# Products, additions and low parts of a hybrid attention and S5 layer given from VectorE to GpSimd, two squares to ScalarE, and a new order list

## The chip, the cores and the metric

The kernel runs on one core of a Trainium2 chip. A core has five engines, each with its own instruction stream, worked through strictly in order: TensorE (PE in the profile; its weight loads are PEld), VectorE (DVE), ScalarE (ACT), GpSimd (POOL) and SyncE (SP), which here does nothing but start transfers. [...] The metric is the device time of one execution in microseconds (us), median of several runs.

## The reference

One decoder layer over a sequence of 1024 tokens with a model width of 1024, all in 32-bit floats.

```python
mod = silu(c) @ w_ada + b_ada                      # shift, scale, gate
h = rms_norm(x, norm_g) * (1 + scale) + shift
proj = h @ w_in     # q | k, v of three branches | z_a | branch gates | u | z_s
q = rms_norm(q, q_norm_g)
kc = rms_norm(compress(k...)); vc = compress(v...)  # gelu(blocks @ w1) @ w2
# three branches per head: compressed keys, selected blocks, window of 512
attn = g0 * softmax(q kc) vc + g1 * softmax(rope(q) ks) vs + g2 * softmax(rope(q) kw) vw
attn = attn * silu(z_a)
y = gelu(s5_mixer(u, ...))                          # complex diagonal recurrence
ssm = y * sigmoid(y @ glu_w + glu_b) * silu(z_s)
out = x + gate * (concat([attn, ssm]) @ w_out)
```

There are 8 heads of 64 in two key groups. With 16 blocks of 64 tokens and 16 of them chosen, every block is chosen, so the selected branch is plain causal attention.

## The kernel before

The tokens are cut into 8 tiles of 128. The work is a set of jobs (several hundred calls of a few dozen functions), and every job records its instructions per engine instead of issuing them. All of them leave through one helper, `issue` (L371), so every row of the profile shows L372; a row is told by its tile, not by its line. Which instruction comes next is fixed by hand: the string `ORD` (L27) lists job, engine letter and count (`hc37:v` is the next VectorE instruction of head 7 of token tile 3; `p a v g s` are TensorE, ScalarE, VectorE, GpSimd, SyncE), and the loop at L1942 issues them in that order. The list thus sets the order on each engine's own stream and of the transfers that an engine starts. The table `FLG` gives some jobs' instructions to one engine or another, and the strings of `SLOTS` say which buffer of a kind each tile takes, in order of use.

The stages, as they lie in time:

- **Start, 0 to 40 us.** Tiles 0 to 3 of x (`x_72` in the order, jobs `xl_0`) and 4 to 7 (`x_73`, jobs `xl_1`) are loaded by SP. Their squares (`x_squares`, L541) are summed, on VectorE or ScalarE as `FLG` says; `x_rstd` (L549) makes the factor of 4 tiles, `x_scale` (L555) multiplies the rows, and TensorE transposes them (`ptr<-ident,x`). Beside this, `mod_chunk` (L533) multiplies a row block of `w_ada`, 128x1024 (`wada<-wada,sc`, jobs `ma`, `mb`), with silu(c) and sums it on VectorE: 16 such products make shift and scale, after which `h_chunk` (L593) makes h in a high and a low part (`hhi`, `hlo`). The weights of w_in are split in the same way (`wh` high part on ScalarE, `wl` low part). `kvaw`, `kva` are weights and matmuls of the keys and values (`wsp`, `ptp`), `cU` and `u..m` those of the S5 input (`wr`, `wh`, `wl`, `pu`).
- **40 to 400 us.** Projections, compressed keys and values (`hid`, `pcp`), the tables and the scan of S5 (`s5p`, `mats`, `scan`), the projection of q with its norm and its rotation: `rope` (L721) makes two products of a half tile with cos and with sin (`ropeb<-qnl,rq`, 128x512) on VectorE and their difference and sum on GpSimd (`qr<-ropeb`).
- **Attention, from about 280 us on.** The tiles go in the order 0, 1, 2, 3, 7, 6, 5, 4 (`OA`, `OB`; 4 is the last). For a head `head_a` (L1511) has scores on TensorE (`S`), the maximum on VectorE (`st<-S`), the exponential on ScalarE with its sum (`pp<-S,st`). Per two heads, `head_s` (L1566) takes the reciprocal of the sums and multiplies by the branch gates (`st<-st,gcol`, 128x4), both on VectorE. `head_b` (L1573) writes the high part of the scaled weights (`hl<-pp,st`, ScalarE), `head_c` (L1584) the low part (`hl<-pp,st,hl`, VectorE), and SP then starts the transposing transfer (`PT<-hl`). `unit_b` (L1609) multiplies with the values (`po<-V,PT`). `cmp_attn` (L1462) is the compressed branch (`Sc`, `hlc`, partly on GpSimd). `attn_trans` (L1647) makes the low part of the gated attention on GpSimd (`oh<-za,oh`).
- **The S5 gate, some 400 to 450 us.** `glu` (L1333) has 8 pieces: a matmul, a tanh, a load of z_s, one VectorE product and a last one that writes with a strided view (`ps<-tg,zz`, 128x512), on VectorE too. `levels` (L1388) then scales `ps` and `attn_out` may follow.
- **Output.** `out_half` (L1668), 16 times: load of half a tile of x (`xo<-in_x`, 128x512), `po` times gate on VectorE (`o<-po,macc,gate`), addition of x (`o<-o,xo`), store by SP. `FLG` puts 14 of the 16 additions on VectorE and two (`ao21`, `ao40`) on GpSimd. `last_halves` (L1705) does it for the last tile, 4, at the very end.

## Time and profile before

| | before |
|---|---|
| median of 3 runs | 634.07 us (631.87, 634.07, 638.18) |
| profiled execution | 633.32 us |
| its span (first to last instruction) | 631.5 us, mean granted clock 0.988 |
| PE busy | 582.0 us, 92% |
| DVE busy | 519.2 us, 82% |
| ACT busy | 397.2 us, 63% |
| POOL busy | 121.1 us, 19% |

Rows give starts and lengths in us from the start of the span. In a view of waits a row names the waiting engine and its output tile, then the engine and tile that released it, then us in total, times and longest. In a group of instructions the last columns are busy us in total, mean ns of one, and the idle time of the engine just ahead of them with what ended most of it. "SPq" and "POOLq" are the streams that start transfers.

### The profile page before, as it was taken

What the parts mean: (1) busy time and instruction counts of PE and PEld (TensorE: products, weight loads), DVE (VectorE), ACT (ScalarE), POOL (GpSimd) and SP (SyncE); (2) the same over time, 40 slices, a digit from 0 to 9 for tenths busy, and PEclk for the clock granted to TensorE, in tenths of its full rate; (3) what the DMA queues carried; (4) which work ended last, traced back from release to release, by engine and by line L of the source; (5) the groups of instructions that cost most, each with busy time, mean ns of one, the idle gap of its engine ahead of it and who ended that gap; (6) DMA issues with size and microseconds to landing.
All of it is one profiled execution on the core that took longest, in us unless ns stands there. A gap on an engine that the chain in (4) does not pass through costs nothing.

```text
span 631.5 us, 12501 instructions
## 1 busy us (share of the span) xinstructions
PE 582.0 (92%) x4615; PEld 427.1 (68%) x4615; DVE 519.2 (82%) x1050; ACT 397.2 (63%) x776; POOL 121.1 (19%) x158
## 2 busy tenths in 40 slices
PE   2599999999999999999999999976999998999893
PEld 0378887788889877888887766545456666556561
DVE  5899896979945686987978899979888989887863
ACT  3586533457443235545989998769857777876750
POOL 0114143121392000333121002001111102010200
PEclk9999999999999999999999999998799999999998
DMA  8999223344566525354656799999999999999996
GB/s 316 385 354 256 49 74 114 91 150 115 154 156 218 161 46 138 114 147 166 175 138 153 165 201 214 214 234 281 241 191 210 256 202 220 188 208 206 219 194 213
DMA packets 211695, 118.85 MB, mean 188 GB/s; under 512 B 159601, under 2 KB 189041, under 8 KB 211634
## 3 DMA queue, kind: packets, MB, share of 16 engines
q1 hardware_dynamic: 208706, 113.05, 73.9%
q0 software_dynamic: 2928, 5.00, 3.6%
q8 instruction: 36, 0.59, 0.4%
q14 instruction: 25, 0.20, 0.1%
HBM read 57.05 MB, written 17.56 MB: 118 GB/s over the span
## 4 chain that ended last, share of the span: by engine, by line
PE 67%; DMA 13%; DVE 11%; ACT 3%; issue 3%; SPq 2%; POOL 0%; POOLq 0%; ACTq 0%; DVEq 0%
PE pcp L372 21%; PE ptp L372 13%; PE po L372 12%; DMA PT<-hl 6%; PE S L372 6%; DVE st L372 2%; PE py L372 2%; PE ph L372 2%; DVE hl L372 2%; SPq L372 2%; PE pk L372 2%; PE pu L372 1%; ACT hl L372 1%; PE pc L372 1%; PE pg L372 1%
## 5 line engine op out<-in xcount | busy, mean ns | idle before, releaser
L372 DVE SCALAR_TENSOR_TENSOR hl<-pp,st,hl 128x640 f16<-128x640 f32 (+7 forms) x128 | 95.3, 765 | 17.4 <-ACT hl L372 16.3
L372 ACT ACTIVATE hl<-pp,st 128x640 f16<-128x640 f32 (+7 forms) x128 | 89.8, 731 | 25.5 <-DMA PT<-hl 11.4
L372 ACT ACTIVATE pp<-S,st 128x640 f32<-128x640 f32 (+7 forms) x128 | 88.7, 697 | 25.2 <-DVE st L372 15.3
L372 PE MATMUL po<-wo,oh 128*128 128x512 f16 x384 | 91.4, 379 | 4.1 <-DVE o L372 2.3
L372 DVE TENSOR_REDUCE st<-S 128x1 f32<-128x640 f32 (+7 forms) x96 | 84.1, 883 | 5.5 <-PE S L372 4.8
L372 PE MATMUL pcp<-hhi,wh 128*128 128x512 f32 x208 | 85.5, 411 | 0.0
L372 PE MATMUL ptp<-wsp,hhi 128*128 128x512 f32 x256 | 83.3, 407 | 0.0
L372 PE MATMUL pcp<-hlo,wh 128*128 128x512 f32 x208 | 82.0, 394 | 0.0
L372 PE MATMUL pcp<-hhi,wl 128*128 128x512 f32 x208 | 81.9, 394 | 0.0
L372 PE MATMUL S<-kT,qg 128*128 128x512 f16 (+3 forms) x384 | 74.6, 319 | 2.1 <-ACT pp L372 2.1
L372 PEld LDWEIGHTS <-PT 128*128 128x128 f16 x1584 | 60.4, 99 | 19.0 <-DMA PT<-hl 8.0
L372 PE MATMUL po<-V,PT 128*128 128x64 f16 x1584 | 66.6, 194 | 6.3 <-DMA PT<-hl 6.3
L372 PEld LDWEIGHTS <-oh 128*128 128x128 f16 x384 | 34.7, 98 | 38.9 <-issue 4.0
L372 PEld LDWEIGHTS ptp<-wsp,hhi 128*128 128x128 f32 x256 | 47.5, 192 | 10.0 <-issue 0.2
L372 PE MATMUL ptp<-wsp,hlo 128*128 128x512 f32 x128 | 50.9, 400 | 0.0
L372 PEld LDWEIGHTS <-qg 128*128 128x128 f16 x384 | 31.7, 99 | 24.9 <-issue 10.4
L372 PEld LDWEIGHTS pcp<-hhi,wh 128*128 128x128 f32 x208 | 39.1, 188 | 9.4 <-issue 0.5
L372 PEld LDWEIGHTS pcp<-hlo,wh 128*128 128x128 f32 x208 | 39.0, 188 | 9.3
L372 PEld LDWEIGHTS pcp<-hhi,wl 128*128 128x128 f32 x208 | 39.2, 188 | 7.6
L372 POOL DMA_DIRECT2D yd<-Y x32 | 19.9, 627 | 89.4 <-ACT Y L372 89.4
L372 POOL TENSOR_TENSOR qr<-ropeb 128x256 f32<-128x256 f32 x16 | 13.2, 844 | 110.8 <-PE S L372 42.2
L372 PE MATMUL S<-dmask,identb 128*128 128x128 bf16 x160 | 29.1, 222 | 4.6 <-ACT pp L372 4.4
(347 smaller groups left out, 1116.9 us busy)
## 6 DMA issues: line engine op xcount, KB each, us to landing
wada<-in_w_adaT_dram SPq DMA_DIRECT2D x24, 512.0 KB, 7.1
wr<-in_w_in_dram SPq DMA_DIRECT2D x14, 512.0 KB, 5.0
x<-in_x_dram SPq DMA_DIRECT2D x8, 512.0 KB, 5.8
...
```

Source lines behind the costliest of these rows:

```text
L372: op(*now(a), **{n: now(x) for n, x in k.items()})
```

## The change

Five kinds of VectorE instructions go to GpSimd, two go to ScalarE, and the list is rewritten:

- `rope`: the second of the two products (with sin) of q, 8 instructions of 128x512; k keeps both on VectorE.
- `glu`: the last product, 8 instructions of 128x512.
- `head_s`: the product with the gates, 32 instructions of 128x4. The reciprocal ahead of it stays on VectorE.
- `head_c`: for the window branch of heads 1, 3, 5, 7 of tile 3, one VectorE instruction becomes two of GpSimd (a scaling in place, then a subtraction).
- `out_half`: the additions of x are on GpSimd for all tiles but the last, and on VectorE for the last. Before, 14 were on VectorE and 2 on GpSimd; now it is 2 and 14.
- `FLG`: the squares of tiles 0 and 2 of x go from VectorE to ScalarE.
- `ORD` and `SLOTS` are new from the first line to the last. Counted in the list, VectorE has 957 instructions for 1023, GpSimd 222 for 154, ScalarE 615 for 613; TensorE has 4321 and SP 432 both times.

```diff
-pre:v kvaw0:s pre:s xl_1:s s5l:s2 pre:s2 kvaw0:a pre:s sc1:p pre:s kvaw0:g pre:s mb0:s s5p:v2 cmpk:s sc1:a s5p:v2 sq4:a
...
-    qw0="d", qw1="d", qw2="d", qw3="d", qw4="d", qw5="d", qw6="t", qw7="d", sq0="d", sq1="a", sq2="d", sq3="d",
+    qw0="d", qw1="d", qw2="d", qw3="d", qw4="d", qw5="d", qw6="t", qw7="d", sq0="a", sq1="a", sq2="a", sq3="d",
...
-            tt(dve, v(cb_[:, k]), v(a.rearrange("p h d -> p (h d)")), x.to_broadcast([128, m, n, d]), OP.mult)
+            tt(pool if k and d == 64 else dve, v(cb_[:, k]), v(a.rearrange("p h d -> p (h d)")), x.to_broadcast([128, m, n, d]), OP.mult)
...
-        tt(dve, o, v(tg), v(zz), OP.mult)
+        tt(pool, o, v(tg), v(zz), OP.mult)
...
-        tt(dve, o, o, gcol[:, i, 3 * h:3 * h + 6].rearrange("p (h b) -> p h b", b=3)[:, :, 1:3], OP.mult)
+        tt(pool, o, o, gcol[:, i, 3 * h:3 * h + 6].rearrange("p (h b) -> p h b", b=3)[:, :, 1:3], OP.mult)
...
+    LOWS = {(3, h, 1) for h in range(1, 8, 2)}
...
-            stt(hl[:, W:2 * W], pp[:, :W], st[br], hl[:, :W], OP.mult, OP.subtract)
+            if (i, h, br) in LOWS:
+                ts(pool, pp[:, :W], pp[:, :W], st[br], None, OP.mult)
+                tt(pool, hl[:, W:2 * W], pp[:, :W], hl[:, :W], OP.subtract)
+            else:
+                stt(hl[:, W:2 * W], pp[:, :W], st[br], hl[:, :W], OP.mult, OP.subtract)
...
-        tt({"p": pool, "d": dve}[FLG.get(f"ao{i}{n}", "d")], o[:], o[:], xo[:], OP.add)
+        tt(dve if i == OB[-1] else pool, o[:], o[:], xo[:], OP.add)
```

**The start.** On VectorE, the stretch up to the factor of the first half of x (`vtmp` is its first step, `ss` the sums of squares; `sm_`, `nn` are small tiles of the S5 parameters; `sc` is silu(c)). Before:

```order
L372 SCALAR_TENSOR_TENSOR sq,ss<-x_72 128x1024
L372 SCALAR_TENSOR_TENSOR sm_166<-sm_166,sm_161 128x16 x4
L372 TENSOR_SCALAR nn<-sm_154 128x16
L372 TENSOR_SCALAR nn<-nn 128x16
L372 TENSOR_TENSOR nn<-sm_154,nn 128x16
L372 SCALAR_TENSOR_TENSOR sq,ss<-x_72 128x1024
L372 SCALAR_TENSOR_TENSOR sc<-sc,pcb 128x512
L372 SCALAR_TENSOR_TENSOR sq,ss<-x_72 128x1024
L372 SCALAR_TENSOR_TENSOR wada,macc<-wada,sc 128x1024
L372 TENSOR_SCALAR vtmp<-ss 128x4
```

After:

```order
L372 SCALAR_TENSOR_TENSOR sc<-sc,pcb 128x512
L372 SCALAR_TENSOR_TENSOR sm_174<-sm_174,sm_167 128x16 x5
L372 TENSOR_SCALAR nn<-sm_160 128x16
L372 TENSOR_SCALAR nn<-nn 128x16
L372 TENSOR_TENSOR nn<-sm_160,nn 128x16
L372 SCALAR_TENSOR_TENSOR sq,ss<-x_72 128x1024
L372 TENSOR_SCALAR vtmp<-ss 128x4
L372 TENSOR_SCALAR mod<-ng 128x8
L372 TENSOR_SCALAR rstd<-vtmp 128x4
L372 SCALAR_TENSOR_TENSOR sc<-sc,pcb 128x512
L372 SCALAR_TENSOR_TENSOR rsq<-rstd 128x4
```

Two squares and a product of `w_ada` no longer stand ahead of `vtmp`; one square is left.

On SP, the first loads, from the third on. Before:

```order
L372 DMA x_73<-in_x_dram 128x1024
L372 DMA dsk<-in_ssm_d_dram 16x32
L372 DMA s5p<-in_s_a_dram 128x48
L372 DMA ident<-in_ident_dram 128x128
L372 DMA x_72<-in_x_dram 128x1024 x4
L372 DMA wada<-in_w_adaT_dram 128x1024
L372 DMA pos<-in_pos_k_dram 128x16
L372 DMA wada<-in_w_adaT_dram 128x1024
L372 DMA wraw<-in_w_in_dram 128x512
```

After:

```order
L372 DMA wraw<-in_w_in_dram 128x512
L372 DMA ident<-in_ident_dram 128x128
L372 DMA x_72<-in_x_dram 128x1024
L372 DMA dsk<-in_ssm_d_dram 16x32
L372 DMA s5p<-in_s_a_dram 128x48
L372 DMA x_72<-in_x_dram 128x1024 x3
L372 DMA bada<-in_b_ada_dram 128x24
L372 DMA wada<-in_w_adaT_dram 128x1024
```

The first tile of the second half of x (`x_73`) no longer stands ahead of the first half, and the second weight tile (`wraw`) comes first instead of behind two blocks of `w_ada`. Further down, the weight of the first S5 column (`wr`, job `cU0`) stands behind 10.07 MB of loads, 10.21 MB before. On TensorE, 24 matmuls of `kva0` and `kva1` stand ahead of the first that needs this weight, 18 before.

**GpSimd in the attention of tile 3 and after.** Before, its stream there has the compressed branch (`Sc`, `hlc`), the rotation (`qr`) and the low parts `oh`:

```order
L372 TENSOR_TENSOR Sc<-Sc,lc 128x512 x2
L372 TENSOR_TENSOR hlc<-Sc,hlc 128x512
L372 TENSOR_TENSOR qr<-ropeb 128x8x32 x2
L372 TENSOR_TENSOR hlc<-Sc,hlc 128x512
L372 TENSOR_TENSOR qr<-ropeb 128x8x32 x2
L372 TENSOR_TENSOR Sc<-Sc,lc 128x512
L372 TENSOR_TENSOR hlc<-Sc,hlc 128x512
L372 TENSOR_TENSOR qr<-ropeb 128x8x32 x2
L372 TENSOR_TENSOR Sc<-Sc,lc 128x512
L372 TENSOR_TENSOR hlc<-Sc,hlc 128x512
L372 TENSOR_TENSOR oh<-za,oh 128x512 x2
```

After, in the same part of the program:

```order
L372 TENSOR_SCALAR pp<-pp,st 128x512
L372 TENSOR_TENSOR hl<-pp,hl 128x512
L372 TENSOR_TENSOR ropeb<-qnl,rq 128x512
L372 TENSOR_TENSOR qr<-ropeb 128x8x32 x2
L372 TENSOR_TENSOR st<-st,gcol 128x4
L372 TENSOR_TENSOR ps<-tg,zz 128x4x8x16
L372 TENSOR_TENSOR Sc<-Sc,lc 128x512
L372 TENSOR_TENSOR hlc<-Sc,hlc 128x512
L372 TENSOR_TENSOR st<-st,gcol 128x4
L372 TENSOR_SCALAR pp<-pp,st 128x512
L372 TENSOR_TENSOR hl<-pp,hl 128x512
L372 TENSOR_TENSOR ps<-tg,zz 128x4x8x16
```

Products of the gates (`st`), low parts (`pp`, `hl`), second table products (`ropeb`) and the last products of `glu` (`ps`) now stand between the others.

**The end.** VectorE's last instructions of the last tile. Before, one addition of this tile is on GpSimd and does not show here; the three that do are two of earlier tiles and the second half's:

```order
L372 SCALAR_TENSOR_TENSOR za<-za,macc,pat 128x128
L372 TENSOR_TENSOR oh<-za,oh 128x128
L372 TENSOR_TENSOR o<-o,xo 128x512
L372 SCALAR_TENSOR_TENSOR o<-po,macc,gate 128x512 x2
L372 TENSOR_TENSOR o<-o,xo 128x512 x2
```

After:

```order
L372 SCALAR_TENSOR_TENSOR za<-za,macc,pat 128x128
L372 TENSOR_TENSOR oh<-za,oh 128x128
L372 SCALAR_TENSOR_TENSOR o<-po,macc,gate 128x512
L372 TENSOR_TENSOR o<-o,xo 128x512
L372 SCALAR_TENSOR_TENSOR o<-po,macc,gate 128x512
L372 TENSOR_TENSOR o<-o,xo 128x512
```

Each half's addition now stands right behind its product, and the earlier tiles' additions are gone. SP's stream at this place is, as before, `xo`, store, `xo`, store for the two halves of the last tile.

## Rows read from the trace of the kernel before

**Rows 1.** The page of the profile: busy time, share of the span and number of instructions of each engine; then the granted clock of TensorE and the mean busy share of the 16 DMA engines, in tenths, over 40 equal slices of the span.
```profile
PE 582.0 (92%) x4615; PEld 427.1 (68%) x4615; DVE 519.2 (82%) x1050; ACT 397.2 (63%) x776; POOL 121.1 (19%) x158
...
PEclk9999999999999999999999999998799999999998
DMA  8999223344566525354656799999999999999996
```

**Rows 2.** Busy time by stretch; each line: stretch in us, busy us (and instructions) of PE, PEld, DVE, ACT and POOL, granted clock, DMA share, GB/s.
```profile
0.00:40.00 40.00, 19.69 (x67) 12.57 (x68) 31.36 (x87) 22.03 (x32) 7.44 (x9) 1.00 0.97 362
40.00:400.00 360.00, 359.73 (x2221) 288.76 (x2220) 298.24 (x666) 218.63 (x479) 86.58 (x125) 1.00 0.58 150
400.00:460.00 60.00, 49.90 (x482) 29.06 (x481) 51.11 (x88) 48.22 (x77) 4.81 (x5) 0.91 1.04 239
460.00:620.00 160.00, 150.76 (x1843) 96.17 (x1842) 133.93 (x205) 108.04 (x191) 20.99 (x18) 1.00 1.11 212
620.00:632.00 12.00, 1.90 (x9) 0.58 (x7) 4.56 (x7) 0.30 (x1) 1.26 (x1) 0.79 0.55 193
```

**Rows 3.** What PE waited for from 395 us to the end: engine, tile, who released it: us in total, times, longest.
```profile
PE po L372 <- DMA PT<-hl: 6.3, 9, 1.8
PE S L372 <- ACT pp L372: 6.2, 5, 1.8
PE pat L372 <- DMA A<-ad: 2.8, 1, 2.8
```

**Rows 4.** What ACT waited for in the same stretch, with the same columns.
```profile
ACT pp L372 <- DVE st L372: 14.0, 19, 2.0
ACT hl L372 <- DMA PT<-hl: 9.9, 7, 4.5
ACT hl L372 <- DVE st L372: 8.8, 9, 1.8
```

**Rows 5.** What SP's queue, which issues most transfers, waited for in the same stretch.
```profile
SPq L372 <- DVE hl L372: 20.2, 10, 4.6
```

**Rows 6.** Groups of VectorE's instructions, each shape apart: output<-inputs, shapes, count | busy us in total, mean ns of one | idle before.
```profile
L372 DVE SCALAR_TENSOR_TENSOR hl<-pp,st,hl 128x512 f16<-128x512 f32 x16 | 11.4, 743 | 0.0
L372 DVE TENSOR_TENSOR ropeb<-qnl,rq 128x512 f32<-128x512 f32 x16 | 10.6, 684 | 0.0
L372 DVE TENSOR_TENSOR o<-o,xo 128x512 f32<-128x512 f32 x14 | 10.1, 728 | 3.7 <-DMA xo<-in_x_dram 3.7
...
L372 DVE TENSOR_TENSOR ps<-tg,zz 128x512 f32<-128x512 f32 x8 | 8.7, 1086 | 0.5 <-DMA zz<-zsd 0.5
...
L372 DVE TENSOR_TENSOR st<-st,gcol 128x4 f32<-128x4 f32 x32 | 5.3, 165 | 0.5
...
L372 DVE SCALAR_TENSOR_TENSOR sq<-x 128x1024 f32<-128x1024 f32 x3 | 3.6, 1216 | 0.0
```

**Rows 7.** Groups of GpSimd's instructions by shape, with the columns of the group before.
```profile
L372 POOL TENSOR_TENSOR Sc<-Sc,lc 128x512 f32<-128x512 f32 x8 | 8.9, 1119 | 47.5 <-DVE st L372 21.7 <-DVE lc L372 16.0 <-ACT wo L372 9.7
...
L372 POOL TENSOR_TENSOR o<-o,xo 128x512 f32<-128x512 f32 x2 | 2.5, 1268 | 34.2 <-DVE o L372 24.7 <-DMA PT<-hl 9.5
...
L372 POOL COPY G<-pos 128x8 f32<-128x8 f32 x4 | 1.7, 440 | 0.0
...
L372 POOL TENSOR_SCALAR s5c<-s5c 128x256 f32<-128x256 f32 x1 | 0.4, 414 | 5.1 <-DMA s5c<-in_s_bc_dram 5.1
```

**Rows 8.** One group of ScalarE's instructions by shape, with the same columns.
```profile
L372 ACT ACTIVATE sq<-x 128x1024 f32<-128x1024 f32 x5 | 5.3, 1057 | 6.2 <-DMA x<-in_x_dram 6.0
```

**Rows 9.** Instructions in order of time at the start: start and length in us, engine, operation, tiles, shapes, count [idle before <-releaser].
```profile
11.04 1.22 DVE L372 SCALAR_TENSOR_TENSOR sq<-x 128x1024 f32<-128x1024 f32 x1
...
20.84 0.75 DVE L372 TENSOR_SCALAR x<-x,rstd 128x1024 f32<-128x1024 f32 x1
...
21.65 1.04 PE L372 MATMUL ptr<-ident,x 128*128 128x128 f32 x2 [10.85 <-DVE x L372]
...
26.74 1.58 DVE L372 SCALAR_TENSOR_TENSOR wada<-wada,sc 128x1024 f32<-128x1024 f32 x1 [0.63 <-DMA wada<-in_w_adaT_dram]
...
30.09 1.09 PE L372 MATMUL ptp<-wsp,hhi 128*128 128x512 f32 x4
...
31.06 1.05 ACT L372 CAST wh<-wr 128x1024 fp32r<-128x1024 f32 x1 [1.84 <-DMA wr<-in_w_in_dram]
...
33.42 0.50 PE L372 MATMUL pu<-hhi,wl 128*128 128x512 f32 x1 [0.42 <-DVE wl L372]
```

**Rows 10.** Instructions in order of time at the end of the span, with the same columns.
```profile
621.39 0.68 DVE L372 TENSOR_TENSOR o<-o,xo 128x512 f32<-128x512 f32 x1
...
622.06 1.41 DVE L372 SCALAR_TENSOR_TENSOR o<-po,macc,gate 128x512 f32<-128x512 f32 x2
622.10 2.41 SPq L372 DMA_DIRECT2D out_dram<-o  x2
622.89 1.26 POOL L372 TENSOR_TENSOR o<-o,xo 128x512 f32<-128x512 f32 x1 [24.67 <-DVE o L372]
623.39 1.31 DVE L372 TENSOR_TENSOR o<-o,xo 128x512 f32<-128x512 f32 x1
624.61 0.38 SPq L372 DMA_DIRECT2D xo<-in_x_dram  x1
...
627.91 0.69 DVE L372 TENSOR_TENSOR o<-o,xo 128x512 f32<-128x512 f32 x1 [3.21 <-DMA xo<-in_x_dram]
```

More of the change, by code (lines that the diff above doesn't have):

```diff
@@ L278 @@
[L278 to L282 removed]
+kvaw1:s pre:s kvaw0:s pre:s2 s5l:s2 kvaw1:a pre:s2 kvaw1:v pre:s pre:v kvaw0:a lb:s sc0:p ma0:s kvaw0:g lb:s s5p:v2
@@ new lines @@
+ub60:p4 ub61:p6 ao31:p2 qt50:s ao31:p ca6:a ao31:p hs65:v hc63:v ao31:p ao21:s ao31:p ub77:p qt50:s ub77:p4 ha67:v
+hs65:g ub77:p ao31:p2 hb64:a ao31:p hc63:s ao31:p3 hb65:a ha66:p hc64:v ha66:p5 ao31:p2 ha67:a ao31:p ha66:v hc62:s
+ao31:p3 qr4:v ub77:p4 ub60:p6 ao30:p2 hc65:v hb64:a ao30:p hc64:s ao30:p3 so6:a ha67:p ca6:v qr4:g ha67:p2 so7:a
+ha67:p2 hc64:v ha67:p ao30:p2 ha66:a ao30:p2 ha67:v qr4:g ao30:p hc64:s ao30:p ao31:p2 so7:v ha67:a ao31:p3 ao30:v
+hc65:s ao31:p hb65:a ub63:p hs67:v ub63:p5 ub72:p2 hs67:g ao31:v ub72:p ub63:p5 hb66:a ub63:p ha50:p4 hc65:v ha50:p
@@ L283 @@
+ub45:p6 ub43:a ub45:p12 ub44:p2 ub43:v ub44:p4 ub46:p12 ub45:p3 ub44:p3 ub45:p2 ao50:s ub45:a ub45:p3 ao31:s ub45:p
+ao30:s ub45:p2 lo:s ub45:p2 ao60:s ub45:p2 ao61:s ub45:p ub46:p7 ub45:v ub46:p11 ub47:p ub45:a ub47:p5 ub46:p2 ao50:g
+ub46:p ub47:p29 ao51:s ub47:a ub45:v ub47:p5 ub47:v ub47:a ub47:v lo:p5 lo:v lo:p ao51:g lo:v lo:s2 ao50:s ao51:s lo:v2
+lo:s
 """.split()
@@ L316 @@
+    mm="0100001010101010101001000101010100010011010101011011101010010110100000100001000001101110",
     w2s="01",
+    b="0123220313",
+    a="01233123022301",
+    pos="01",
     pbh="01",
     mc="00101010",
-    st="01012013203120132013201320132103",
-    lc="01001011",
-    f2="01234562706612707045621035641245707345671027610572504653",
+    st="01203021301230123012302103210321",
+    lc="01010100",
+    f2="01234256104201072416506323027105642753041067264071043060",
     p4="01234567")
```

527 lines of the change are left out of this document (257 added, 270 removed).

## The prediction

> **What bounds the kernel now.** First the page: busy time by engine, then the granted clock and the DMA share [rows 1]. TensorE (PE) is busy for 582.0 of 631.5 us, so 49.5 us of the span is all that other engines could give back if every wait of PE went away. VectorE (DVE) is second with 519.2, GpSimd (POOL) has 121.1, 19%. So the change relieves the second engine, not the first, and only counts where PE stands still.
>
> Where that is, the windows show [rows 2]. From 40 to 400 us PE is busy for 359.73 of 360 us: a quicker DVE is worth nothing there. PE stands still for 40 - 19.69 = 20.3 us at the start, 10.1 from 400 to 460 (where the clock is 0.91, so at most 0.09 x 60 = 5.4 more by the clock), 9.2 from 460 to 620 and 10.1 at the end. The DMA share is 0.97 at the start, 1.04 and 1.11 in the last two long stretches: there the transfers are loaded as well.
>
> Then who releases whom from 395 us on. PE waits 6.3 us for transposes `PT` and 6.2 for exponentials `pp` [rows 3]. ScalarE's `pp` in turn waits 14.0 us for maxima `st` from DVE [rows 4], and SP, which starts the transposes, waits 20.2 us for low parts `hl` from DVE [rows 5]. DVE is therefore two steps ahead of PE in both chains, and this is what the change can shorten.
>
> **What DVE loses.** From the groups [rows 6]: 12 additions of x net, at 0.728 us, are 8.7; 8 products of `rope` at 0.684 are 5.5; 8 last products of `glu` at 1.086 are 8.7; 32 gate products at 0.165 are 5.3; 4 low parts at 0.743 are 3.0; 2 squares at 1.216 are 2.4. In all 33.6 us of 519.2.
>
> **What GpSimd gets.** An addition of this shape costs it 1.268 us and a product 1.119 [rows 7]: 12 x 1.27 = 15.2 and 8 x 1.12 = 9.0. The strided `glu` product is not shown there. Its bounds are 1.12 (as any product) and 1.27 x 1.086/0.684 = 2.0 (slowed as on DVE); I take 1.5 midway, 12 us. The 128x4 product lies between DVE's 0.165 and the 0.44 of a 128x8 copy; I take 0.3, 9.6 us. A low part is now a scaling, about 2 x 0.414 for twice the shown 256 columns, and a subtraction of about 1.2: 2.0, four times 8 us. Together some 54 us, so POOL goes to about 175, 28%. It is no bound by its sum. ScalarE gets 2 x 1.06, at a moment when it waits for x (6.0 us over its squares) [rows 8].
>
> **What two engines cost each other.** At the end a DVE addition of 0.68 us took 1.31 beside a POOL addition [rows 10]: 0.63 us, about half of the POOL instruction, came on top. I charge each large POOL instruction beside a loaded DVE with this 0.63. One row is thin; the bounds are 0 (no overlap) and 1.27 (DVE held for the whole POOL instruction). There are 36 large ones among those that moved (12 additions, 8 products of `rope`, 8 of `glu`, 8 of low parts): 36 x 0.63 = 22.7 us come back to DVE by the row, 36 x 1.27 = 45.7 by the upper bound, which is more than the 33.6 it loses.
>
> [...]
>
> **Start (term -2.4).** TensorE's first transposes of x wait 10.85 us for the first scaling, at 20.84 on DVE [rows 9]. Ahead of it two squares (2 x 1.22) and one product of `w_ada` (1.22) drop out, 3.66 us in all, if DVE is what is late. But DVE itself waits there for loads (0.63 us for `wada` at 26.74), and the DMA share is 0.97 [rows 2, 9]. Next comes the weight of the first S5 column: its high part on ScalarE waits 1.84 us for the transfer, and PE 0.42 for the low part. In the new list it stands behind nearly the same bytes, so it lands no earlier, but six more matmuls of 1.09/4 = 0.27 us stand ahead of it and fill 1.6 us that were idle. Bounds 0 (transfers set the pace for everything) and -3.66. Between the 1.6 that PE fills anyway and 3.66 I take -2.4, nearer to the lower because the transfers are loaded.
>
> **40 to 400 us (term 0).** Here PE is full. The adds, rotations and gate products that leave DVE shorten nothing. The cover is PE's own work, 359.73 of 360 us; where a stall of POOL outlasts it the price is in the second rival.
>
> **400 to 460 us (term -3).** Here lie the eight `glu` products (8.7 us of DVE), the low parts (3.0), a rotation (0.7), some six gate products (1.0) and about one addition (0.7): 14 us. Some 17 large POOL instructions replace them; at 0.63 that is 10.7 back. Net 3.3, taken as -3, and it reaches PE through `pp` [rows 3, 4]. Bounds 0 and -12, the second being what PE can gain at all (10.1 idle, and 2 of the clock's 5.4).
>
> **460 to 620 us (term -1.2).** About ten additions, one rotation and fifteen gate products leave DVE: 7.3 + 0.7 + 2.5 = 10.5 us. Some 12 large POOL instructions give 7.6 back. Of the net 2.9 I let 1.2 reach PE, since the DMA share is 1.11 and PE waits for the transposes themselves [rows 2, 3]. Bounds 0 and -4.
>
> **End (term -0.7).** In the last tile SP's stream is `xo`, store, `xo`, store. The first half's addition on POOL ends at 622.89 + 1.26 = 624.15; only then may its store go, and behind it the last `xo` at 624.61, which the last addition waits 3.21 us for [rows 10]. With the addition on DVE right behind its product (products end at 622.06 + 0.7 = 622.77) it is done at about 623.44, and everything after comes 0.7 earlier. That is the surest term.
>
> **Hand-over (term +0.3).** A gate product now goes DVE to POOL and back to ScalarE and DVE; where nothing stands ahead of it on POOL that is lost in the waits named.
>
> Sum: -2.4 - 3 - 1.2 - 0.7 + 0.3 = -7.0. The profiled execution took 633.32 with a span of 631.5, so span 624.5 and execution 626.3. It was 0.75 below the median of 634.07; against that the change gives 627.0, 1.1% faster. About 1% is what a measurement of this kernel can tell from no change.
>
> **Rivals.**
>
> *The relief ends in other waits (about 632).* PE in 40 to 400 us stays full, and from 400 on the transposes set the pace at shares of 1.04 and 1.11 [rows 2], or POOL's instructions hold DVE for their whole length and take back all that it was given (45.7 for 33.6 us). Then only 1.6 at the start and 0.7 at the end remain: 634.1 - 2.3 = 632; with the start at 0 as well, 633 to 634. [...] For it: PE's own largest wait late is for `PT` [rows 3]. Against it: these transposes wait in turn for DVE's `hl` [rows 5].
>
> *The gate product in POOL's queue (slower, about 641.5).* POOL works in order. A gate product behind an addition of 1.27 us waits for it, and then both ScalarE's `hl` and DVE's low parts, and all transposes of the two heads, are late. With DVE the product stood right behind its reciprocal. There are 16 such pairs in tiles 7, 6, 5 and 4; if half of 16 x 1.27 = 20.3 us reaches PE, that is +10.2, less 2.7 for start and end: +7.5. It decides from about 0.45 us per pair on, where 16 pairs cost the forecast's whole 7 us. For it: SP already waits 20.2 us for `hl`, ScalarE 9.9 for `PT` [rows 4, 5]. Against it: POOL is busy for only 20.99 of 160 us there [rows 2], some 16 more after the change, so most products would find it free.
>
> *The relief passes in full (about 615).* No lock costs anything and DMA keeps up: -3.7, -12, -4, -0.7 give -20, so 614 to 617. For it: ScalarE waits 14.0 + 8.8 us for DVE [rows 4], DVE waits little. Against it: the DMA shares.
>
> **How the numbers follow.** The forecast, with its own range 622 to 631, gets 0.50: the end is sure, the start likely, the middle rests on one row of the lock. Of that, 0.31 lies below 627.7, which is 1% faster. The relief lost in other waits gets 0.25 and lies within 1%. The gate product in the queue gets 0.14, the full relief 0.11. So faster 0.31 + 0.11 = 0.42, same 0.19 + 0.25 = 0.44, slower 0.14. The range holds the forecast, the lost relief and most of the full one, from 616 to 637; it leaves out most of the slower case and a part of the quickest, together about 2 in 10.
>
> **What would show it.** The start is right if PE's first transposes of x begin 2 to 4 us sooner and its idle time up to 40 us falls below 19. The middle is right if `pp` waits less than 10 us for `st` after 395 and PE's busy share from 400 to 460 rises. The lock is right if DVE's means beside POOL rise, `o<-po,macc,gate` and `hl` above all; it is wrong if they stay. The slower rival shows as waits of ScalarE's `hl` for a POOL `st`, or as SP waiting longer for `hl`. The end is right if the last `xo` is issued within 2 us of the last product. I am wrong in the large if 40 to 400 us is no longer filled by PE, or if its work there grew.

## The result, and the profile after

Over 20 runs of each, the changed kernel took 631.30 us (629.36 to 633.46) and the kernel before 635.71 (631.87 to 639.38, and one of 1722.28). The ratio of the times is 0.9932, with a 95% interval of 0.9914 to 0.9950: 0.7% faster. The forecast was 627.0, or 0.9888 of the median it started from: the sign and the range hold, but its gain of 1.1% lies outside the interval. The profiled execution took 629.77 us with a span of 628.0, 3.5 us less span than before (7.0 were forecast). Everything read from rows below is one execution of each kernel.

The page after, with the lines that answer to [rows 1]:

```profile
PE 584.8 (93%) x4615; PEld 429.0 (68%) x4615; DVE 499.6 (80%) x982; ACT 398.9 (64%) x780; POOL 183.5 (29%) x226
...
PEclk9989999999999999999999999998899998999998
DMA  8996344255455742437565889999989999999997
```

DVE lost 19.6 us, not the 33.6 that the lengths of its moved rows add up to. PE itself became 2.8 us busier, with the same number of matmuls: some of them ran at a slower pace (0.42 us each instead of 0.23, at the start), and the clock row shows a dip in the third slice (31 to 47 us) that it did not have before. In the four runs below that leave the start of the new list as it is (experiments 4 and 7, and the second run of 6), PE is busy for 581.5 to 585.5 us, so this is not in every execution.

Busy time by stretch after, columns as in [rows 2]:

```profile
0.00:40.00 40.00, 21.45 (x66) 12.78 (x67) 30.31 (x84) 23.50 (x35) 8.00 (x9) 0.99 0.96 355
40.00:400.00 360.00, 359.20 (x2208) 289.13 (x2207) 287.82 (x638) 218.35 (x478) 107.33 (x153) 1.00 0.57 149
400.00:460.00 60.00, 50.81 (x501) 30.18 (x500) 48.80 (x79) 48.24 (x78) 21.44 (x19) 0.94 1.05 247
460.00:620.00 160.00, 153.38 (x1845) 96.88 (x1843) 130.55 (x184) 108.83 (x191) 45.51 (x45) 0.99 1.10 216
620.00:632.00 12.00, 0.00 (x0) 0.00 (x0) 2.10 (x3) 0.00 (x0) 1.26 (x1) 0.70 0.35 121
```

PE's idle time (stretch less busy) fell by 1.8 us up to 40 us, rose by 0.5 from 40 to 400, fell by 0.9, then by 2.6, and from 620 to the end of the span by 1.6 (8.0 for 9.6). That is 6.4 of idle time less, against 2.8 of busy time more.

These stretches hold different work in the two kernels, so I also compared the times at which the same amount of work was done. Each matmul counts with the median distance from its start to the next one's, for its shape in the trace, and the sum is PE's position, in us of work. How late the changed kernel is, against the one before, at the same position (the kernel before reaches 20, 60, 380 and 440 us of work at 36, 77, 401 and 476 us of its span, and the lag hardly moves from 456 to 476):

```
work done (us)          20     60    380    440   PE's last   span's end
after, lag in us     -1.27  +2.50  +2.11  -0.11     -2.94        -3.5
stage:            start +2.5; 60-380 -0.4; 380-440 -2.2; 440 to PE's last -2.8; tail -0.6
forecast:         start -2.4;         0 ;          -3  ;                  -1.2;      -0.7
```

So the first transposes did come sooner, and by 60 us of work more than all of it was lost: the start is 4.9 us off its forecast. That is more than the whole error of 3.5 us. The 2.50 is one execution's: the four runs that leave this start as it is are 5.06, 2.68, 4.40 and 3.05 us late there, and the four with the old list (experiments 5 and 8, and the first run of 6) 0.14 to 1.30. The loss is there each time, some 3 us on average, but two single lags must lie 2 to 3 us apart to tell anything.

Who releases whom from 395 us on, after, columns as in [rows 3, 4, 5]:

```profile
PE S L372 <- ACT pp L372: 7.5, 7, 2.8
...
ACT hl L372 <- POOL st L372: 6.9, 8, 1.3
...
ACT pp L372 <- DVE st L372: 5.3, 9, 1.1
```

```profile
SPq L372 <- DVE hl L372: 14.9, 10, 4.6
```

The waits for DVE that the prediction named did shrink: `pp` for maxima from 14.0 to 5.3 us, SP for low parts from 20.2 to 14.9. PE's own wait for `pp` did not: it is 7.5 us for 6.2. ScalarE waits 6.9 us for the gate products on GpSimd, the trace of the slower rival; before, it waited 8.8 us for them on DVE [rows 4].

The start, PE's rows after:

```profile
20.12 1.32 PE L372 MATMUL ptr<-ident,x 128*128 128x128 f32 x3 [8.04 <-DVE x L372]
...
38.32 0.50 PE L372 MATMUL pu<-hlo,wh 128*128 128x512 f32 x1 [1.28 <-DVE hlo L372]
...
39.32 1.20 PE L372 MATMUL ptp<-wsp,hhi 128*128 128x512 f32 x2
...
42.92 0.63 PE L372 MATMUL ptp<-wsp,hhi 128*128 128x512 f32 x2
...
55.54 0.50 PE L372 MATMUL pu<-hlo,wh 128*128 128x512 f32 x1 [0.77 <-DMA hlo<-hf]
```

And what DVE and GpSimd do ahead of the wait at 38.32:

```profile
34.76 1.82 DVE L372 TENSOR_SCALAR x<-x,rstd 128x1024 f32<-128x1024 f32 x1
36.50 1.77 DVE L372 TENSOR_TENSOR hlo<-hf,hhi 128x512 fp32r<-128x512 f32 x1
```

```profile
34.73 1.29 POOL L372 TENSOR_TENSOR hlo<-hf,hhi 128x512 fp32r<-128x512 f32 x1 [5.76 <-DVE rstd L372]
35.98 1.74 POOL L372 TENSOR_TENSOR wsp<-wraw,wsp 128x512 fp32r<-128x512 f32 x1
```

The first transposes begin 1.53 us sooner (20.12 for 21.65). But PE then waits 1.28 us for a low part that DVE makes in 1.77 us. Beside GpSimd's first instruction DVE's scaling, and beside its second the low part, end 0.56 and 0.55 us behind GpSimd's. Behind that wait the matmuls go slowly: the eight from 39.32 up to 42.68 take 0.42 us each, those from 42.92 on 0.23, a loss of 1.5 us. The granted clock is 0.90 from 35 to 40 us and 0.76 from 40 to 45; before it was 1.00 in both. The four other runs with this start have the same wait (1.27 or 1.28 us), but only one of them such a clock (0.87 and 0.79); in three it stays at 1.00 in both. At 55.54 follows a second wait, for a low part that a DMA of GpSimd's queue finishes. In the kernel before, PE had none of this; its only wait between 34 and 60 us is this one:

```profile
39.11 0.44 PE L372 MATMUL ptr<-ident,x 128*128 128x128 f32 x2 [0.82 <-DVE x L372]
```

It is for the second half of x, which DVE scaled from 35.57 to 39.05. After the change the same scalings run from 34.76 to 38.92. So what is late next, once the first half of x comes sooner, is its second half, and that did not come sooner.

Instructions that moved, and those that can feel it, columns as in [rows 6, 7]:

```profile
L372 DVE SCALAR_TENSOR_TENSOR o<-po,macc,gate 128x512 f32<-128x512 f32 x16 | 11.9, 746 | 4.9 <-PE po L372 2.7 <-DMA out_dram<-o 2.2
L372 DVE SCALAR_TENSOR_TENSOR hl<-pp,st,hl 128x512 f16<-128x512 f32 x12 | 11.0, 927 | 0.2 <-ACT hl L372 0.2
```

```profile
L372 POOL TENSOR_TENSOR o<-o,xo 128x512 f32<-128x512 f32 x14 | 20.7, 1484 | 36.5 <-PE po L372 14.1 <-DMA xo<-in_x_dram 11.4 <-DVE o L372 11.0
...
L372 POOL TENSOR_TENSOR ropeb<-qnl,rq 128x512 f32<-128x512 f32 x8 | 12.0, 1506 | 40.5 <-ACT s5tab L372 9.9 <-DVE mc L372 8.9 <-DMA s5T<-Kt 8.0
L372 POOL TENSOR_TENSOR ps<-tg,zz 128x512 f32<-128x512 f32 x8 | 11.1, 1396 | 16.2 <-DVE tg L372 9.7 <-DMA zz<-zsd 4.1 <-DVE macc L372 2.4
L372 POOL TENSOR_TENSOR st<-st,gcol 128x4 f32<-128x4 f32 x32 | 8.9, 278 | 92.8 <-DVE st L372 81.5 <-DMA glw<-in_glu_w_dram 7.2 <-DVE lc L372 4.1
...
L372 POOL TENSOR_SCALAR pp<-pp,st 128x512 f32<-128x512 f32 x4 | 6.4, 1603 | 3.6 <-DMA PT<-hl 2.1 <-ACT hl L372 1.5
L372 POOL TENSOR_TENSOR hl<-pp,hl 128x512 f16<-128x512 f32 x4 | 4.9, 1235 | 0.3
```

A low part `hl` of 512 columns rose on DVE from 743 to 927 ns; the last product `o<-po,macc,gate` stayed, 746 for 744. GpSimd pays as well: its addition takes 1.48 us for 1.27.

The end, VectorE's and SP's instructions in order of time:

```profile
619.96 0.69 DVE L372 TENSOR_TENSOR o<-o,xo 128x512 f32<-128x512 f32 x1
...
621.10 0.38 SPq L372 DMA_DIRECT2D xo<-in_x_dram  x1
...
622.81 0.75 DVE L372 SCALAR_TENSOR_TENSOR o<-po,macc,gate 128x512 f32<-128x512 f32 x1 [2.16 <-DMA out_dram<-o]
624.36 0.69 DVE L372 TENSOR_TENSOR o<-o,xo 128x512 f32<-128x512 f32 x1 [0.79 <-DMA xo<-in_x_dram]
```

The first half's addition stands right behind its product, and the last `xo` goes out at 621.10. But the second product now waits 2.16 us for a buffer that an earlier store has not let go of, and the addition 0.79 for `xo`.

### The profile page after: what moved, and what is told of

The parts are those of the page before. It is cut to its first block, busy times and chain, and to the rows that moved or that the text cites. A ratio compares the mean times of both kernels' runs of the same rounds, so it can differ in the third digit from the quotient of the medians.

```text
span 628.0 us, 12517 instructions
## 1 busy us (share of the span) xinstructions
PE 584.8 (93%) x4615; PEld 429.0 (68%) x4615; DVE 499.6 (80%) x982; ACT 398.9 (64%) x780; POOL 183.5 (29%) x226
## 4 chain that ended last, share of the span: by engine, by line
PE 62%; DMA 7%; issue 2%; ACT 1%; DVE 1%; POOL 0%; SPq 0%; ACTq 0%; DVEq 0%
PE po L372 17%; PE pcp L372 16%; PE S L372 9%; PE ptp L372 6%; DMA PT<-hl 4%; PE pglu L372 4%; PE ph L372 2%; DMA wor<-in_w_out_dram 2%; PE py L372 2%; PE pc L372 2%; PE pg L372 1%; PE pk L372 1%; DMA PTc<-hlc 1%; PE pqc L372 1%; ACT pp L372 1%
## 5 line engine op out<-in xcount | busy, mean ns | idle before, releaser
L372 DVE SCALAR_TENSOR_TENSOR hl<-pp,st,hl 128x640 f16<-128x640 f32 (+7 forms) x124 | 98.7, 817 | 7.0 <-ACT hl L372 6.2
L372 PE MATMUL ptp<-wsp,hhi 128*128 128x512 f32 x256 | 84.7, 413 | 0.0
L372 PE MATMUL po<-V,PT 128*128 128x64 f16 x1584 | 64.9, 194 | 6.1 <-DMA PT<-hl 3.2
L372 POOL TENSOR_TENSOR st<-st,gcol 128x4 f32<-128x4 f32 x32 | 8.9, 278 | 92.8 <-DVE st L372 81.5
L372 DVE SCALAR_TENSOR_TENSOR wada<-wada,sc 128x1024 f32<-128x1024 f32 x24 | 29.9, 1263 | 5.3 <-DMA wada<-in_w_adaT_dram 5.3
```

The lines of the kernel that those rows point to most:

```text
L372: op(*now(a), **{n: now(x) for n, x in k.items()})
```

## The experiments

The theory after the result: the late stretches gain what the moves give, in the new order only, and the start loses it again through low parts that come late and through the second half of x. The rivals: the moves are good anywhere and the list does nothing; the list alone is the gain; the gate products on GpSimd cost what is missing. In the quoted texts each letter has the meaning that its own text gives it. Ratios are to the kernel before on the same chip, in five rounds. "PE at 60 us" and the like is the lag of the table above, at 60 us of work, from one execution of each run. Each ratio rests on 5 to 12 executions of the changed program.

**1. The late low part sooner.** The low part `h30` stands ahead of the first scaling of the second half of x in the list, instead of behind it (the list is shown here and below in parts of lines):

```diff
-kvaw2:a h20:g xsc1:v u1m:p u2m:p xsc1:a u2m:p tb:s h30:v u2m:p
+kvaw2:a h20:g h30:v xsc1:v u1m:p u2m:p xsc1:a u2m:p tb:s u2m:p
```

> The new kernel with one VectorE instruction put two places further forward in the list: the low part of h of the fourth row block (hlo<-hf,hhi) goes ahead of the two scalings of the second half of x. Theory A (the start was lost at one wait): in the new kernel PE waits 1.28 us for this low part at 37.0 us, and the granted clock is 0.76 to 0.90 from 35 to 45 us right after; with the low part first the wait falls under 0.4 us, the clock stays at 1.00, and the run comes out 2 to 3 us under the new kernel, ratio to before about 0.989. Rival B (the start doesn't reach the end, or the clock fell for another reason): PE's wait goes but the time stays at 0.992 to 0.994.

631.39 us, ratio 0.9918 [0.9887, 0.9949], no different from the change. PE's waits between 34 and 60 us in this run:

```profile
36.62 0.49 PE L374 MATMUL pu<-hlo,wh 128*128 128x512 f32 x1 [0.65 <-POOL hlo L374]
...
38.87 0.44 PE L374 MATMUL ptr<-ident,x 128*128 128x128 f32 x2 [0.83 <-DVE x L374]
...
55.77 0.80 PE L374 MATMUL pu<-hlo,wh 128*128 128x512 f32 x1 [2.67 <-DMA hlo<-hf]
```

The wait of 1.28 us is gone, the clock stays at 1.00 from 35 to 55 us, and the wait for x is back where it was before the change. But the low part by DMA here ends a wait of 2.67 us, though it was issued 1.67 us sooner (48.57 for 50.24): it landed 7.2 us after its issue, for 5.3. Behind that wait the clock is 0.51 from 55 to 60 us, and PE at 60 us is 5.55 late. The longer wait is not the edit's doing. With the start untouched it is 2.68, 2.63 and 2.65 us in experiment 4, the second run of 6 and the first of 7, where the transfer went out at 48.57 to 49.31 us; the second of these runs shows

```profile
55.73 0.50 PE L374 MATMUL pu<-hlo,wh 128*128 128x512 f32 x1 [2.63 <-DMA hlo<-hf]
```

In the second run of 7, issued at 50.23, it is 1.32. In all six the matmul that needs the low part starts between 55.5 and 56.6 us, whenever the transfer went out. So the edit takes away the first of two waits for low parts, the wait for x takes its place, and the second is left. By 440 us of work the lag is down to 1.09, against -0.11 in the change: a start that is 3.0 us later in its execution is 1.2 later there. A late start is partly absorbed behind.

**2. Both low parts.** As in 1, and `h50` is made on DVE in one instruction instead of a copy on ScalarE and the adding DMA:

```diff
-h50="t"
+h50="d"
...
-u0m:p2 h50:a u0m:p mb7:v xb31:p2 h50:g xb31:p2
+u0m:p2 h50:v u0m:p mb7:v xb31:p4
```

> The new kernel with its start mended in two places: the low part of the fourth row block ahead of the scalings of the second half of x, and the low part of the sixth block (first half of the tokens) by one VectorE subtraction at a place where VectorE stood idle for 4 us, instead of a ScalarE copy and an adding transfer by GpSimd's queue. Theory A (the start term failed because PE, sooner at the matmuls that need these two low parts, waits there, and the clock falls after such a wait): no wait of PE over 0.5 us for a low part before 60 us, clock 1.00 from 30 to 65 us, PE 3 to 5 us ahead of the new kernel at 60 us, of which about half is left at the end (in the run with the low part first, 3.0 us more delay at 60 us left 1.4 at the end): 1.5 to 2.5 us faster than the new kernel, ratio to before 0.989 to 0.991. Rival B (a later wait swallows all of it): ratio 0.993 as the new kernel.

629.33 us, 0.9917 [0.9886, 0.9949], not told apart from the change. No wait for a low part is above 0.64 us, the clock is 1.00 from 30 to 60. PE's first long wait is again the one for x, at the place where it was before the change:

```profile
39.21 0.44 PE L374 MATMUL ptr<-ident,x 128*128 128x128 f32 x2 [1.08 <-DVE x L374]
```

PE at 60 us is 1.79 late, for 2.50 to 5.06 with the start untouched. With the low parts out of the way the second half of x is what PE waits for next, as in the kernel before; one longer wait follows, 1.39 us at 53.71 for `hf` from ScalarE.

**3. The second half of x as well.** As in 2, and both scalings of the second half on DVE stand right behind their factor, with `h30` and one product of `w_ada` behind them; the two instructions `mc6` also go ahead of `h50`:

```diff
-h30:a rstd1:v ma4:v h30:a tb:s
+h30:a rstd1:v h30:a tb:s
...
-rstd1:v mb6:s u1m:p rstd1:v u1m:p kvaw2:a h20:g xsc1:v
+rstd1:v mb6:s u1m:p rstd1:v xsc1:v2 h30:v ma4:v u1m:p kvaw2:a h20:g
```

> The new kernel with the mended start (both low parts) and three more moves in VectorE's list: the two scalings of the second half of x right behind the last step of its factor, a product of w_ada behind them, and the columns of the seventh block ahead of the sixth block's low part. Theory A (the second half of x sets the start: PE waits for its scaling at 39.1 us in the kernel before and at 39.2 with the first mending, whatever the first half does): PE gets the second half at 37.0 to 37.8 us, has no wait over 0.5 us from 40 to 60, is 1 to 1.5 us ahead of the kernel before at 60 us, and ends 1 to 2 us sooner than the first mending, ratio to before 0.988 to 0.991. Rival B (the gate stage, which waits for ScalarE, VectorE and transposes, swallows it): the same time as the first mending, 0.992.

628.65 us, 0.9882 [0.9862, 0.9902]: the best of all, 1.2% faster than before. The interval does not meet that of the change; it does meet that of experiment 2. DVE's scalings, and PE's busy time where the change dipped:

```profile
33.82 1.42 DVE L374 TENSOR_SCALAR x<-x,rstd 128x1024 f32<-128x1024 f32 x2
```

```profile
35.00:40.00 5.00, 4.52 (x22) 3.31 (x21) 5.00 (x5) 4.30 (x6) 3.33 (x3) 1.00 1.05 409
40.00:45.00 5.00, 4.24 (x24) 3.32 (x23) 5.00 (x13) 4.10 (x7) 0.00 (x0) 1.00 1.02 341
```

Both scalings are done at 35.24 instead of 38.92, the wait for x at 39 us is gone, the clock is whole, and PE at 60 us is 0.35 ahead of the kernel before. So the start stops losing once the second half of x is moved too. The 2.4 us that the term promised are not reached even then.

**4. The list alone.** The new list, with all moved instructions back on VectorE (the squares stay on ScalarE):

```diff
-            tt(pool if k and d == 64 else dve, v(cb_[:, k]), v(a.rearrange("p h d -> p (h d)")), x.to_broadcast([128, m, n, d]), OP.mult)
+            tt(dve, v(cb_[:, k]), v(a.rearrange("p h d -> p (h d)")), x.to_broadcast([128, m, n, d]), OP.mult)
...
-        tt(pool, o, v(tg), v(zz), OP.mult)
+        tt(dve, o, v(tg), v(zz), OP.mult)
...
-        tt(pool, o, o, gcol[:, i, 3 * h:3 * h + 6].rearrange("p (h b) -> p h b", b=3)[:, :, 1:3], OP.mult)
+        tt(dve, o, o, gcol[:, i, 3 * h:3 * h + 6].rearrange("p (h b) -> p h b", b=3)[:, :, 1:3], OP.mult)
...
-    LOWS = {(3, h, 1) for h in range(1, 8, 2)}
+    LOWS = set()
...
-        tt(dve if i == OB[-1] else pool, o[:], o[:], xo[:], OP.add)
+        tt(pool if (i, n) == (2, 1) else dve, o[:], o[:], xo[:], OP.add)
```

> The new list and the two squares on ScalarE, but all products, low parts and additions that went to GpSimd are back on VectorE at the same places of the list (the addition of x in the last tile is on VectorE in both). Theory A (the relief of VectorE is worth the 2.3 us found from 400 to 456 us and the 3.1 after that, and the new list by itself loses 2.5 at the start): about 5 us over the new kernel, 636 to 638, ratio to before 1.000 to 1.004. Rival B (the new order, not the engines, brought the gain): the same time as the new kernel, ratio 0.993.

637.51 us, 1.0007 [0.9982, 1.0031]. The list by itself gives nothing. DVE is busy for 516.6 us, so in this list the moves take 17.0 us off it, where the lengths of their rows (without the squares) add up to 31.2. PE's lag is 5.06 us at 60, 8.15 at 380 and 5.59 at 440: in the stage from 380 to 440 it gains 2.6 us with no instruction moved, as much as the change (2.2).

**5. The moves alone.** The old list and the old squares, with the five kinds of instructions on GpSimd at the places where they stood (the code lines are those of the change, and in the list only the engine's letter changes):

```diff
-        tt(dve, o, v(tg), v(zz), OP.mult)
+        tt(pool, o, v(tg), v(zz), OP.mult)
...
-        tt({"p": pool, "d": dve}[FLG.get(f"ao{i}{n}", "d")], o[:], o[:], xo[:], OP.add)
+        tt(dve if i == OB[-1] else pool, o[:], o[:], xo[:], OP.add)
```

> The list of the kernel before with the engine letters alone changed: second table products of q, last products of the S5 gate, gate products, four low parts and the additions of x go to GpSimd at their old places, the last tile's addition to VectorE; squares stay. Theory A (the start of the new list is a loss, the relief a gain): start as before, the late gain of 5 us kept in part, ratio 0.991 to 0.994. Rival B (moves need the new order, since a GpSimd instruction takes twice as long and stands in the way at its old place): ratio 0.997 to 1.005, with ScalarE waiting over 10 us for a gate product of GpSimd.

638.33 us, 1.0037 [1.0014, 1.0059]: slower than before. Neither half gives anything alone (+0.07% and +0.37%), both together -0.68%. DVE's busy time and ScalarE's longest wait for GpSimd:

```profile
PE 587.1 (92%) x4615; PEld 430.4 (68%) x4615; DVE 508.8 (80%) x986; ACT 397.5 (63%) x776; POOL 182.0 (29%) x226
```

```profile
ACT hl L374 <- POOL st L374: 11.2, 8, 2.6
```

At the old places DVE's busy time falls by 10.4 us instead of 17.0, ScalarE waits 11.2 us for gate products, and `pp` still waits 13.9 for maxima. From 380 to 440 us of work PE gains nothing (1.90 and 1.89).

**6. The gate products.** Once as in 5, with the gate products left on VectorE:

```diff
-        tt(pool, o, o, gcol[:, i, 3 * h:3 * h + 6].rearrange("p (h b) -> p h b", b=3)[:, :, 1:3], OP.mult)
+        tt(dve, o, o, gcol[:, i, 3 * h:3 * h + 6].rearrange("p (h b) -> p h b", b=3)[:, :, 1:3], OP.mult)
```

> The list of the kernel before with the engine letters changed as in the run of the moves alone, but the 32 gate products left on VectorE. Theory A (at the old places the gate products stand behind long GpSimd instructions, and ScalarE's 11.2 us of waiting for them makes the loss): 3 to 4 us faster than the moves alone, ratio to before 0.997 to 0.999. Rival B (the loss comes from the other moves, which delay what waits for them): ratio stays at 1.002 to 1.005.

637.32 us, 1.0039 [1.0017, 1.0060]. The wait of 11.2 us is gone and nothing comes of it (ScalarE now waits 10.9 for the same products on DVE). And once the same edit in the changed kernel:

> The new kernel with the 32 gate products of 128x4 back on VectorE. Theory A (the hand-over is paid in ScalarE's waits, 6.9 us for GpSimd's st, which hide behind others): within 0.2% of the new kernel, the waits of ScalarE for st going back to VectorE. Rival B (the hand-over costs): 1.5 to 3 us faster than the new kernel, ratio under 0.990. Rival C (VectorE's 5.3 us count): 1 to 2 us slower, ratio 0.995.

633.64 us, 0.9952 [0.9927, 0.9976]. The interval overlaps that of the change: if anything the gate products help there. With them on DVE, here and in experiment 4, PE is busy for only 17.8 and 17.7 us of the 20 from 380 to 400, for 20.0 in the change. The slower rival's wait exists, but it isn't what the change pays with.

**7. The additions, and the `glu` products.** The changed kernel, with its 13 additions of earlier tiles back on VectorE:

```diff
-        tt(dve if i == OB[-1] else pool, o[:], o[:], xo[:], OP.add)
+        tt(pool if (i, n) == (2, 1) else dve, o[:], o[:], xo[:], OP.add)
```

> The new kernel with 13 additions of x back on VectorE (the last tile's are there in both, one of tile 2 stays on GpSimd). Theory A (the additions are the greater part of the gain after 460 us): 2 to 3 us slower than the new kernel, all of it after 456 us, ratio to before 0.996 to 0.998. Rival B (additions are off the chain that PE waits for): under 0.8 us slower, ratio 0.993.

633.85 us, 0.9984 [0.9959, 1.0008], whose interval does not meet that of the change. The additions are worth 0.5% or 3.3 us, most of the gain. At 440 us of work this run is 1.45 late, at the end of the span 1.7: it gains nothing more from there on, where the change gains 3.4 (its profiled execution took 635.05 us, 1.2 above the run's median). With the eight last products of `glu` back instead:

```diff
-        tt(pool, o, v(tg), v(zz), OP.mult)
+        tt(dve, o, v(tg), v(zz), OP.mult)
```

> The new kernel with the 8 last products of the S5 gate back on VectorE. Theory A (they make the gain from 400 to 456 us): PE 1.5 to 2.5 us later at 456 us than in the new kernel, ratio to before 0.995 to 0.997. Rival B (the stage waits for ScalarE and the transposes whatever VectorE does): within 0.5 us, ratio 0.993.

632.07 us, 0.9951 [0.9927, 0.9975], not told apart from the change; PE at 440 us of work is 0.46 ahead of before, where the change is 0.11 ahead. The `glu` products, the largest item of the term for 400 to 460, are not seen to bring anything.

**8. Which moves lose at the old places.** As in 5, with only the additions moved:

```diff
-        tt({"p": pool, "d": dve}[FLG.get(f"ao{i}{n}", "d")], o[:], o[:], xo[:], OP.add)
+        tt(dve if i == OB[-1] else pool, o[:], o[:], xo[:], OP.add)
```

> The list of the kernel before with only the additions of x moved to GpSimd (the last tile's to VectorE). Theory A (relief without a new order becomes idle time of VectorE, whatever is moved; the loss of the moves at the old places lies in the products): ratio 0.998 to 1.001. Rival B (the additions are what loses, as they hold VectorE's low parts for 1.27 us each): 1.003 or more.

635.40 us, 0.9988 [0.9973, 1.0004], and with only rotations, `glu` products and low parts moved:

```diff
-        tt(dve, o, v(tg), v(zz), OP.mult)
+        tt(pool, o, v(tg), v(zz), OP.mult)
...
+    LOWS = {(3, h, 1) for h in range(1, 8, 2)}
```

> The list of the kernel before with the second table products of q, the last products of the S5 gate and the four low parts moved to GpSimd, additions and gate products left on VectorE (the last tile's addition is on VectorE). Theory A (these make the loss: a gate product of 1.5 us and a low part of 2.8 us late for what waits for them): ratio 1.002 to 1.005. Rival B (additions make it): 0.998 to 1.001.

637.43 us, 1.0018 [0.9998, 1.0037]. The additions do no harm there and little good, the products tend to the slower side. The loss is not settled on one of them.

**9. What two engines cost each other, by itself.** A small kernel that computes nothing of the reference, in one execution: six instructions of DVE alone, then twelve beside six additions of GpSimd, for five kinds of DVE instruction.

```diff
+        for f in (d_two, d_low, d_psum, d_red, d_one):
...
+            for _ in range(6):
+                f()
+            meet(outs[f], 1)
+            for _ in range(12):
+                f()
+            for _ in range(6):
+                g_two()
+            meet(outs[f], 2)
```

Here `f` is an addition of two tiles in SBUF, a low part, a product that reads PSUM, a maximum over PSUM, or a scaling of 1024 columns; `g_two` is GpSimd's addition of 128x512; at `meet` the two engines wait for each other.

> A small kernel for the price of the lock alone; it computes nothing of the layer (its output is a copy of x with a few columns overwritten). Five forms of VectorE instruction, each 6 times alone and 12 times beside 6 additions of 128x512 on GpSimd: an addition of two tiles in SBUF, the low part with its 16-bit operand, the product with an operand in PSUM (as o<-po,macc,gate), the maximum over PSUM (as st<-S), and the scaling of 128x1024 by a column (as x<-x,rstd). Theory A (an instruction that reads two operands in SBUF, or the quick scaling, waits until GpSimd's is over; one that reads PSUM doesn't): additions, low parts and scalings take turns with GpSimd's, so the stretch lasts about the sum of both, GpSimd's mean goes from 1.26 to 1.7 us or more; products and maxima with PSUM keep their 0.74 and 0.69 us and GpSimd its 1.26. Rival B (half a GpSimd instruction is lost on average, whatever the form, as I charged with 0.63): all five forms grow by 0.3 us or more in the mean.

DVE's rows, the six alone and the twelve beside GpSimd: an addition of two tiles in SBUF, a product that reads PSUM (`p`), and a scaling with one input in SBUF.

```profile
15.66 4.32 DVE L53 TENSOR_TENSOR vc<-va,vb 128x512 f32<-128x512 f32 x6
...
21.68 13.37 DVE L53 TENSOR_TENSOR vc<-va,vb 128x512 f32<-128x512 f32 x12
...
59.36 4.67 DVE L56 SCALAR_TENSOR_TENSOR vc<-p,vs,vb 128x512 f32<-128x512 f32 x6
...
65.72 9.39 DVE L56 SCALAR_TENSOR_TENSOR vc<-p,vs,vb 128x512 f32<-128x512 f32 x12
...
93.83 4.69 DVE L62 TENSOR_SCALAR vw<-vw,vs 128x1024 f32<-128x1024 f32 x6
...
100.21 13.81 DVE L62 TENSOR_SCALAR vw<-vw,vs 128x1024 f32<-128x1024 f32 x12
```

GpSimd's six additions, beside the first kind and alone:

```profile
20.48 9.67 POOL L68 TENSOR_TENSOR pc<-pa,pb 128x512 f32<-128x512 f32 x6
...
114.52 7.96 POOL L68 TENSOR_TENSOR pc<-pa,pb 128x512 f32<-128x512 f32 x6
```

Twelve additions alone would be 8.64 us; they took 13.37. The first of GpSimd's six ran ahead of them, from 20.48 on, so five cost DVE 4.73 us, 0.95 each, and themselves (9.67 - 7.96)/5 = 0.34. One by one:

```profile
20.48 1.26 POOL L68 TENSOR_TENSOR pc<-pa,pb 128x512 f32<-128x512 f32 x1
20.56 1.19 DVE L76 TENSOR_TENSOR vr<-tok 128x3 f32<-128x3 f32 x1 [0.39 <-POOL tok L75]
...
23.55 1.59 POOL L68 TENSOR_TENSOR pc<-pa,pb 128x512 f32<-128x512 f32 x1
24.06 1.63 DVE L53 TENSOR_TENSOR vc<-va,vb 128x512 f32<-128x512 f32 x1
```

A DVE addition of three columns, 0.16 us alone (15.58 in this trace), stands until 21.75, when GpSimd's is over (21.74). A DVE addition of 512 columns that begins at 24.06 ends at 25.69, 0.55 us behind GpSimd's (25.14), and that one had in turn begun while the DVE addition before it ran (until 24.02). In these rows the two engines take turns. Twelve products that read PSUM took 9.39 for 9.34: nothing. The low part behaves as the addition (13.80 for 9.36) and the maximum from PSUM as the product (8.65 for 8.62); the scaling, with one input in SBUF, pays like the addition (13.81 for 9.38), five times 1.63 us for 0.75.

## Why the prediction was right and wrong

**Start: wrong, and this is the step that failed.** "Between the 1.6 that PE fills anyway and 3.66 I take -2.4": this priced how much sooner the first half of x comes and asked no further than the first S5 weight. The first transposes came 1.53 us sooner, not the 2 to 4 that I had named, and PE's idle time up to 40 us is 18.6, below the 19 that was asked for; but by 60 us of work PE was 2.5 late, and 2.68 to 5.06 in the other runs with this start. What stands in place of the term: what is late next is the second half of x, whose scaling ends at the same time in both kernels, and two low parts became late that had not been (1.28 us, and 0.77 to 2.68). In two of the five executions PE also worked slowly behind the first of these, 1.5 us in the change. Experiment 2 takes the low parts away and finds x at 39.21; experiment 3 takes x away too, and the start is 0.35 ahead, with 0.5% of the time. My sign "idle time up to 40 us falls below 19" was met while the start was lost: it looked at too short a stretch and at idle time only.

**40 to 400 us: right.** PE is busy for 359.2 of 360 us, and the lag moves by -0.4 from 60 to 380.

**400 to 460: the size about right, the reason wrong.** -2.2 by work, -3 forecast, `pp` waits 5.3 us instead of 14.0, and PE is busy for 50.8 of 60 us instead of 49.9, as the signs asked. But PE's own wait for `pp` grew from 6.2 to 7.5. The list alone gains 2.6 us in the same stage with no move in it, the moves in the old list gain 0.0, and the `glu` products on DVE again lose nothing. So the gain comes with the list. Part of it may be a late start made good (experiment 1), but not all: experiment 3, which is 0.70 ahead at 380, gains 2.5 here too. What in the list does it is not shown.

**460 to 620: under-sized.** -2.8 for -1.2. The reason was right: most of it is the additions (experiment 7), though the list alone, without them, gains 1.2 us from 440 to PE's last. That less came back to DVE than I charged fits this. That the DMA share, 1.10 here, kept less of the relief from PE than I allowed for is a guess.

**What DVE loses, and what two engines cost each other: both over-charged.** ("The lock" in the prediction and the expectations is this price.) The 33.6 us add up lengths of rows, but DVE's rows overlap by some 0.08 us where one follows another: before, all its rows are 578.4 us long and cover 519.2. What the moved instructions alone cover there is some 26 us. So of the 33.6 - 19.6 = 14.0 us about 8 were never to be had and about 6 came back, not 22.7. Where the price is paid, it is more than my 0.63, namely 0.95 (experiment 9). I misread the row at the end: that addition ended 0.55 us behind GpSimd's, so it was held for all that was left of it, and 0.63 only tells how late in GpSimd's instruction it began. But I charged the price to every large GpSimd instruction. In the trace after, only 14 of the 38 rows of the moved kinds hold a DVE instruction up, by 8.4 us together; most of the others run beside DVE instructions that read PSUM, and these keep their length (the commonest, the maximum `st<-S` of 640 columns, 819 ns for 816). I named `o<-po,macc,gate` as the first to show it: it reads PSUM, and stayed at 746 ns (744 before). `hl` showed it, 927 ns for 743. In experiment 9 the addition (13.37 us for 8.64), the low part (13.80 for 9.36) and the scaling (13.81 for 9.38) pay, and the two forms with an input in PSUM don't (9.39 for 9.34 and 8.65 for 8.62). Its rows that stand one by one also show who is held: the addition of three columns begins 0.08 us behind GpSimd's and ends with it, at 21.75 for 21.74.

**End: right in size.** -0.6 for -0.7. Not "everything after comes 0.7 earlier", though: the product now waits for a store's buffer, 2.16 us. (PE's 10.1 us of idle time at the end were counted to 632; the span ends at 631.5, so they are 9.6.)

**GpSimd's sum: right.** 183.5 us for 175. The low part took 2.8 us for the 2.0 taken, the rotation 1.51 for 1.12. GpSimd is held too: in experiment 9 one of its additions took 1.59 us for 1.26.

**What had no term.** PE was 2.8 us busier in this execution, with the same matmuls. The sum was made of waits alone; what PE can lose in pace behind a wait (0.42 us for 0.23 a matmul, 1.5 us in all, at the start) wasn't in it.

**The rivals.** "The relief passes in full" did not happen: the median fell by 4.4 us, not 20. "The relief ends in other waits" is close to the total, but for the wrong reason: the additions' relief did reach PE late, and the start gave part of the gain away. "The gate product in POOL's queue" is visible as a wait of 6.9 us and costs nothing that experiments 4 to 6 can show. That the moves need a new order around them was no rival of mine: at the old places they lose 0.37%.

**Left open.** Why the moves lose at the old places is only partly told: there DVE's busy time falls by 10.4 us, for 17.0 in the new list, and experiment 8 doesn't settle on one kind. The rotations, the low parts and the squares were not undone one by one in the new list. Why the adding DMA lands 5.3 us after its issue in one run and 7.2 in another, at nearly the same time in all, is not explained.
